# Rotating the columns of an 8192 x 8192 fp32 matrix: the wrapped row ends staged through SBUF as 512 B blocks

## The chip, the core and the metric

One NeuronCore of a Trainium2 chip. The time is the device time of one execution in microseconds (us); the figure of a kernel is the median of its runs.

## The reference

`x` is 8192 x 8192 float32, `shift` is 100, and the result is `np.roll(x, shift, axis=1)`: in every row, `out[r, c] = x[r, (c - 100) mod 8192]`. So a row of the output begins with the last 100 elements (400 B) of the input row, and goes on with its first 8,092 (32,368 B). A row is 32,768 B, the matrix 268.4 MB. Nothing is computed; every byte is read once and written once.

## The kernel before

It consists of DMAs from DRAM to DRAM and has no tile in SBUF. With `s = 100` it cuts the 8,192 rows into 16 chunks of 512 rows. For each chunk line 28 issues one DMA of the long pieces, `out[r, 100:] <- x[r, :8092]`: 512 pieces of 32,368 B, one a row. The chunks take turns between the queue of SP (`nc.sync`) and that of ACT (`nc.scalar`), 8 DMAs each. Line 30 issues, on GpSimd's queue, the row ends of the same chunk, `out[r, :100] <- x[r, 8092:]`: 512 pieces of 400 B, 16 DMAs in all.

No two DMAs touch the same bytes, so nothing in the data orders them. The only waits are those by which a semaphore that tells a DMA's completion is used again: the program as built lets four DMAs be outstanding on SP and on ACT and eight on GpSimd, and a later issue waits for the DMA that used its semaphore last. In the output row the long piece starts at byte 400 and ends at the row's end; in the input row it starts at byte 0. The row end starts at byte 32,368 of the input row and byte 0 of the output row.

Of the kernel before, what the change touches and what calls it, by code (L numbers as in the profile page):

```python
# [1 line left out]

# [4 lines left out]


@with_exitstack
def kernel(  # L10
    ctx: ExitStack,
    tc: tile.TileContext,
    x: bass.AP,
    shift: int,
    out: bass.AP,
):
    nc = tc.nc
    n_rows, n_cols = x.shape
    s = shift % n_cols

    engines = [nc.sync, nc.scalar]
    n_chunks = 16
    rows = n_rows // n_chunks
    for i in range(n_chunks):
        r = slice(i * rows, (i + 1) * rows)
        engines[i % 2].dma_start(out=out[r, s:], in_=x[r, :n_cols - s])
        if s > 0:
            nc.gpsimd.dma_start(out=out[r, :s], in_=x[r, n_cols - s:])  # L30


# [1 line left out]
_INS = ['x', 'shift']  # L34
_OUTS = [((8192, 8192), 'float32')]

_NUMBERS = {'shift': 100}


def kernel(**inputs):  # L40
    import numpy as _np
    import concourse.bacc as _bacc
    import concourse.tile as _tile
    from concourse import mybir as _mybir
    from concourse.bass_utils import run_bass_kernel_spmd as _run

    nc = _bacc.Bacc("TRN2", target_bir_lowering=False, num_devices=1)  # L47
    arrays, args = {}, []
    for name in _INS:
        if name in _NUMBERS:  # L50
            args.append(_NUMBERS[name])
            continue
        a = _np.ascontiguousarray(inputs[name])
        if a.dtype.kind in "iu":
            a = a.astype(_np.int64)
        arrays[f"in_{name}_dram"] = a
        args.append(nc.dram_tensor(f"in_{name}_dram", a.shape, _mybir.dt.from_np(a.dtype), kind="ExternalInput").ap())
    for i, (shape, dtype) in enumerate(_OUTS):
        dt = _mybir.dt.from_np(_np.dtype(dtype))
        args.append(nc.dram_tensor(f"out_{i}_dram", shape, dt, kind="ExternalOutput").ap())  # L60
    with _tile.TileContext(nc) as tc:  # L61
        kernel(tc, *args)
    r = _run(nc, [arrays], core_ids=[0])
    got = tuple(r.results[0][f"out_{i}_dram"] for i in range(len(_OUTS)))
    return got[0]
```

## Time and profile before

| what | value |
|---|---|
| median of 5 runs | 831.17 us (830.85 to 843.72) |
| the profiled execution, its own time | 828.21 us |
| its span, first to last instruction | 826.4 us |
| DMA share between 230 and 800 us | 1.00, at 331 GB/s |
| DMA share between 800 and 826.4 us | 0.57, at 232 GB/s |
| issue of a GpSimd DMA (L30) | 0.62 us each, 16 of them, the last at 114.2 us |
| issue to landing, median: SP, ACT, GpSimd | 399.3, 399.0, 107.6 us |

The span is that of one execution; its own time is 1.8 us more, and the median of the runs 4.8 us more. The page gives each DMA queue's share of the 16 DMA engines' time, the share of that time in which they were busy, and the bytes moved per second; GB/s count a copied byte once, though it is read and written. A queue's packet is what an engine takes from it in one turn: one long piece, or several short ones. The packet records of the trace, which the page adds up, give each packet's start, size and duration. "Issue to landing" of a DMA includes its waiting behind those that were issued before it.

### The profile page before, as it was taken

The numbers are of one execution on the slowest core, as the hardware profiler recorded it, in microseconds if no ns is written. First come the engines' busy times: TensorE is split into PE (matmuls) and PEld (weight loads), VectorE is DVE, ScalarE is ACT, GpSimd is POOL, SyncE is SP. The second block draws the span as 40 slices with busy tenths as digits, with TensorE's granted clock in tenths as the row PEclk, the third lists the DMA queues.
The fourth block names the chain that finished last, engine by engine and source line by source line (L and its number), as shares of the span: only waits on it lengthen the run. The fifth ranks groups of instructions, "written<-read, shape, count | busy, mean of one in ns | idle before, by whom it ended". The sixth has DMA issues, their size and how long they took to land. (4 is left out here: it accounts for less than half of the span.)

```text
span 826.4 us, 81 instructions
## 1 busy us (share of the span) xinstructions
POOL 10.2 (1%) x20
## 2 busy tenths in 40 slices
POOL 2000000000000000000000000000000000000000
DMA  9999999999999999999999999999999999999994
GB/s 292 319 319 326 321 314 325 332 318 332 325 331 329 343 327 332 334 321 332 335 323 337 335 331 334 327 335 334 331 332 327 329 332 329 324 326 331 334 323 213
DMA packets 9472, 268.44 MB, mean 325 GB/s; under 512 B 512, under 2 KB 512, under 8 KB 1280
## 3 DMA queue, kind: packets, MB, share of 16 engines
q1 hardware_dynamic: 4224, 132.58, 49.1%
q10 hardware_dynamic: 4224, 132.58, 47.0%
q0 software_dynamic: 1024, 3.28, 2.3%
HBM read 268.44 MB, written 268.44 MB: 650 GB/s over the span
## 5 line engine op out<-in xcount | busy, mean ns | idle before, releaser
L30 POOL DMA_DIRECT2D out_dram<-in_x_dram x16 | 10.0, 630 | 104.4 <-DMA out_dram<-in_x_dram 103.6
L47 POOL MEMSET const-float32-0.0<- 128x1 f32 x1 | 0.1, 98 | 0.2 <-issue 0.2
L47 POOL MEMSET const-bfloat16-1.0<- 128x1 bf16 x1 | 0.1, 101 | 0.0
L47 POOL MEMSET const-float32-1.0<- 128x1 f32 x1 | 0.1, 98 | 0.0
L47 POOL MEMSET const-uint8-127<- 128x1 uint8 x1 | 0.1, 98 | 0.0
## 6 DMA issues: line engine op xcount, KB each, us to landing
out_dram<-in_x_dram SPq DMA_DIRECT2D x8, 16184.0 KB, 399.3
out_dram<-in_x_dram ACTq DMA_DIRECT2D x8, 16184.0 KB, 399.0
out_dram<-in_x_dram POOLq DMA_DIRECT2D x16, 200.0 KB, 107.6
```

The source lines that it names most:

```text
L30: nc.gpsimd.dma_start(out=out[r, :s], in_=x[r, n_cols - s:])
L47: nc = _bacc.Bacc("TRN2", target_bir_lowering=False, num_devices=1)
```

## The change

The long pieces start at the next multiple of 128 elements: with `a = 128` and `g = a - s = 28`, line 31 of the new kernel copies `out[r, 128:] <- x[r, 28:8092]`, 8,064 elements (32,256 B) a row, in the same 16 DMAs on SP and ACT. The first 128 elements of an output row, the 100 wrapped ones and the 28 that stood at the front of the input row, go through SBUF. They lie apart in one input row, but the last 100 elements of row r - 1 and the first 28 of row r are neighbours in memory, so one read of 512 B fetches both. The rows are handled in 8 blocks of 1,024 (128 partitions x 8 rows). For each block GpSimd's queue issues a read of 1,024 such pieces (line 65), and a small read of the end of the eighth row of each partition (line 66); the first block, which has no row ahead of it, reads 1,024 ends of 400 B (line 59) and 1,024 fronts of 112 B (line 61). Two VectorE copies per block (lines 68 and 70) put the end and the front of the same row together in a second tile, and a DMA on GpSimd's queue (line 73) stores 1,024 blocks of 512 B to `out[:, :128]`. Each of the two pools has 8 buffers, as many as there are blocks. In the source the store of block k - 1 comes after the read of block k.

As the program is built, GpSimd's queue holds 25 DMAs in this order: L59, L61, L65, L66, L65, L73, L66, L73, L65, L66, L73, and then L65, L66, L73 for each further block, with the last store at the end. Each L73 waits for VectorE's copies of its block, each copy for the landing of what it reads; from the ninth DMA on, an issue also waits for the DMA eight places ahead of it.

```diff
-    for i in range(n_chunks):
-        r = slice(i * rows, (i + 1) * rows)
-        engines[i % 2].dma_start(out=out[r, s:], in_=x[r, :n_cols - s])
-        if s > 0:
-            nc.gpsimd.dma_start(out=out[r, :s], in_=x[r, n_cols - s:])
+    a = -(-s // 128) * 128
+    g = a - s
+    for i in range(n_chunks):
+        r = slice(i * rows, (i + 1) * rows)
+        if a < n_cols:
+            engines[i % 2].dma_start(out=out[r, a:], in_=x[r, g:n_cols - s])
...
+    m = 8
+    n_st = n_rows // P // m
+    reads = ctx.enter_context(tc.tile_pool(name="reads", bufs=n_st))
+    heads = ctx.enter_context(tc.tile_pool(name="heads", bufs=n_st))
+    xt = x.rearrange("(k p j) c -> k p j c", j=m, p=P)
+    ot = out.rearrange("(k p j) c -> k p j c", j=m, p=P)
+    tiles = []
+    for k in range(n_st + 1):
+        if k < n_st:
+            t = reads.tile([P, m + 1, a], x.dtype)
+            if k == 0:
+                nc.gpsimd.dma_start(out=t[:, 1:, :s], in_=xt[k, :, :, n_cols - s:])
+                if g > 0:
+                    nc.gpsimd.dma_start(out=t[:, :m, s:], in_=xt[k, :, :, :g])
+            else:
+                lead = bass.AP(tensor=x.tensor, offset=k * P * m * n_cols - s,
+                               ap=[[m * n_cols, P], [n_cols, m], [1, a]])
+                nc.gpsimd.dma_start(out=t[:, :m, :], in_=lead)
+                nc.gpsimd.dma_start(out=t[:, m, :s], in_=xt[k, :, m - 1, n_cols - s:])
+            h = heads.tile([P, m, a], x.dtype)
+            nc.vector.tensor_copy(h[:, :, :s], t[:, 1:, :s])
+            if g > 0:
+                nc.vector.tensor_copy(h[:, :, s:], t[:, :m, s:])
+            tiles.append(h)
+        if k > 0:
+            nc.gpsimd.dma_start(out=ot[k - 1, :, :, :a], in_=tiles[k - 1])
```

## The prediction

> **What bounds the kernel now.** I read the page's head and its DMA part first, because no compute engine does anything here.
>
> ```profile
> span 826.4 us, 81 instructions
> ...
> DMA  9999999999999999999999999999999999999994
> GB/s 292 319 319 326 321 314 325 332 318 332 325 331 329 343 327 332 334 321 332 335 323 337 335 331 334 327 335 334 331 332 327 329 332 329 324 326 331 334 323 213
> DMA packets 9472, 268.44 MB, mean 325 GB/s; under 512 B 512, under 2 KB 512, under 8 KB 1280
> ## 3 DMA queue, kind: packets, MB, share of 16 engines
> q1 hardware_dynamic: 4224, 132.58, 49.1%
> q10 hardware_dynamic: 4224, 132.58, 47.0%
> q0 software_dynamic: 1024, 3.28, 2.3%
> HBM read 268.44 MB, written 268.44 MB: 650 GB/s over the span
> ```
>
> The 16 DMA engines are busy from the first slice to the last one. The long pieces (q1 is one of the SP and ACT queues, q10 the other) take 96.1% of the engines' time, the row ends on GpSimd's q0 2.3%. So a long piece costs 0.961 x 826.4 x 16 / 8192 = 1,551 ns, and all row ends together cost 0.023 x 826.4 = 19.0 us of every engine. The sum closes: 0.984 x 826.4 = 813.2 us of work, and 13 us in which an engine has nothing (2 us of start, the rest in the last slices, where the engines end one after the other).
>
> Second, the rate by stage, where the columns are POOL's busy time, the clock, the DMA share and GB/s:
>
> ```profile
> 0.00:114.00 114.00, 9.59 (x19) 1.00 0.99 316
> 114.00:230.00 116.00, 0.62 (x1) 1.00 1.00 324
> 230.00:800.00 570.00, 0.00 (x0) 1.00 1.00 331
> 800.00:826.40 26.40, 0.00 (x0) 1.00 0.57 232
> ```
>
> While row ends are in flight the engines are as busy, but move less: (331-316)/331 x 114 + (331-324)/331 x 116 = 7.6 us are lost, on top of the 9.9 us that 3.28 MB take at 331 GB/s. Together 17.5 us, close to q0's 19.0: the time of small pieces is nearly all added to the end, and only 1.5 to 2 us come back because the long pieces run a little faster beside them.
>
> Third, how GpSimd's ring gets its turns, from the timeline of the issues:
>
> ```profile
> 0.74 214.04 SPq L28 DMA_DIRECT2D out_dram<-in_x_dram  x5
> 0.74 219.62 ACTq L28 DMA_DIRECT2D out_dram<-in_x_dram  x5
> 1.26 5.03 POOL L30 DMA_DIRECT2D out_dram<-in_x_dram  x8 [0.82 <-PEq L61]
> 19.39 0.62 POOL L30 DMA_DIRECT2D out_dram<-in_x_dram  x1 [13.10 <-DMA out_dram<-in_x_dram]
> 33.00 0.62 POOL L30 DMA_DIRECT2D out_dram<-in_x_dram  x1 [12.98 <-DMA out_dram<-in_x_dram]
> ```
>
> One 200 KB DMA completes every 13.6 us. On each engine it is 32 pieces, which the packet records of the trace show as three packets (11, 11 and 10 pieces of 400 B) and a 4-byte completion: four turns, each beside one long piece of either other queue, 2 x 1.55 + 0.3 = 3.4 us. 4 x 3.4 = 13.6. The chain of waits follows POOL only, to 115 us, so it says nothing of the end; the end is the engines' total work.
>
> **What the change does to that sum.** (1) Removed: all sixteen 400 B DMAs, -19.0 us (q0's share).
>
> (2) The long pieces shrink from 32,368 to 32,256 B: 0.35% of 0.961 x 826.4 = 794 us, -2.7 us. They now start at 512 B of the output row instead of 400, but at byte 112 of the input row instead of 0. Does that change their rate? The trace has only the old form. The shortest long packets in its records take 1,199 ns, 27.0 GB/s, with the write at byte 400: an unaligned write alone doesn't hold an engine back. The mean is 1,551 because 16 engines together ask for more than they get. Here the Trainium skill's "HBM Reference" (Specifications) speaks against a gain: it puts a stack at about 716 GB/s. Our row of 331 GB/s is 331 read and 331 written, 662 in total, so by the page at most 716/662 = 8% (about 60 us) is left for any alignment; by the row nothing is shown to be left. Bounds: -60 us, and +16 us (2%) if an unaligned read costs more than an unaligned write did, since the change moves the offset rather than removing it. I take 0, the row's side: both ends of the copy still differ by 400 B.
>
> (3) Added: the reads into SBUF. The first block of 1,024 rows has 1,024 pieces of 400 B and 1,024 of 112 B; seven more have 1,024 of 512 B and 128 of 400 B each: 10,112 pieces, 4.55 MB. (4) Added: 8 stores of 1,024 blocks of 512 B: 8,192 pieces, 4.19 MB. In all 8.75 MB instead of 3.28 and 18,304 pieces instead of 8,192. The old packets closed at about 4 KB, so 8 blocks of 512 B should make one. Per engine the first block is then 6 + 2 packets, the seven others 8 + 1 each, the stores 8 each: 8 + 63 + 64 = 135 packets, instead of 48.
>
> Price of a packet: the nearest row is q0's own: 19.0 us / 48 = 396 ns for 4,267 B on average. The shortest records of that form take 155 to 172 ns, 25.7 GB/s. So 135 packets cost between 135 x 0.165 = 22 us and 135 x 0.385 = 52 us. The excess of about 220 ns arises in a copy with HBM on both sides; a read into SBUF or a store out of it has HBM on one side only. I take half the excess: 165 + 110 = 275 ns, 37 us. A rule speaks for less: the skill's "DMA: Bandwidth & Descriptors" (Specifications) asks for 512 B or more for line rate and says that below it the engine reads, modifies and writes. By that rule the old 400 B were the dear form, and 8.75 MB / 16 at 27.0 GB/s, 20 us, would be the whole new price; the sum would be 19.0 + 2.7 - 20 = 2 us faster. The row doesn't show that penalty: 400 B pieces reach 25.7 GB/s in the shortest packets, and the mean's excess of 220 ns is smaller than the long packets' own, 1,551 - 1,199 = 352 ns. I stay with 37.
>
> (5) Relief: small packets that use HBM on one side leave more of it to the long ones. Before, 19 us of small packets gave back about 2 us. 37 us of packets with half the demand should give back about three times that: 6, so 4 more.
>
> Sum: -19.0 - 2.7 + 37 - 4 = +11 us. Span 826.4 + 11 = 838. The profiled execution's own time was 828.21 and the median of the runs 831.17; the same difference on the median gives 842.
>
> **What I cost at nothing, and its cover.** VectorE's 16 copies have no row before. GpSimd's fills of one element took 0.1 us; an estimate from the 0.96 GHz in the skill's page "VectorE: DVE Perf Modes" (Specifications) is 800 / 0.96 = 0.8 us for the larger copy, up to 15 us in all. GpSimd issues 25 DMAs instead of 16, at 0.62 us for 512 pieces; with twice the pieces up to 1.3 us, some 30 us. Each store waits in GpSimd's queue for the copies of its block, and so for that block's read. Behind the waiting store stands the read two blocks later, and for that VectorE and then the next store wait. This is a chain, but by the built order the next block's reads are already in the ring when a store waits: about 10 turns of work cover the copies. Turns: 135 + 25 completions = 160 x 3.4 = 544 us (the same count gives 64 x 3.4 = 218 for before, where the rows above show the small pieces gone by 230). The long pieces run to about 815 us. So 270 us of cover is left; a stall of 5 us at each of eight stores uses 40 of it. SP and ACT keep their 16 issues and their waits.
>
> **The rivals.** (A) *Hidden anyway, no change.* If HBM alone is the limit, the engine time of the SBUF legs is absorbed: its bytes are unchanged at 537 MB, 811 us at 662 GB/s, plus 10 to 13 us of start and tail: span 822 to 824, median 827 to 829. For it: 662 is near the page's 716, and long packets at 1,199 show that engines could do more. Against it: the 316 row, where small pieces gave back only 2 of 19 us.
>
> (B) *Faster.* The price is hidden in the long pieces' 1,551 ns, at their write starting at byte 400. To come out over 1% faster in spite of the +11, the long pieces must gain 19 of 794 us: from 1,551 to about 1,513 ns. With 4%, 32 us, the time is 810. For it: the mean is far above 1,199. Against it: the unaligned long pieces already move 662 GB/s, and 112 B of offset remain on the read. The alignment then did not do what it says.
>
> (C) *Much slower.* Small packets cost as much as before or more (0.385 us or above): 52 - 19 - 2.7 - 2 = +28, 859. Also here: if a packet held one block, 1,060 turns x 3.2 us would outlast the long pieces, and the ring would end alone, well over 880. The 11-piece packets speak against that.
>
> **How the numbers follow.** The forecast has 0.44 (its own range 836 to 852), A 0.30, B 0.14, C 0.12. A change of 1%, about what a measurement of this kernel can tell from no change, is 823 and 839.5. Faster: B's 0.14, and 0.02 of A that ends below 823: 0.16. Same: the rest of A, 0.28, and 0.06 of the forecast that ends between 836 and 839: 0.34. Slower: 0.38 and C's 0.12: 0.50. For 8 in 10, the range leaves out the stronger half of B and the upper half of C: 815 to 862. The likeliest is 842.
>
> **What would show it.** q0's share near 37/838 = 4.4%: 2.5% supports the rule and A, 6% supports C. q1 plus q10 at 94 to 95% with a rate in the last undisturbed stage of 331: my zero for alignment; 340 or more is B, 325 or less an unaligned read that costs. The last store's issue near 500 to 550 us; after 800 it would be C's chain. VectorE under 2% busy. I am wrong if the long pieces' rate moves by over 1% either way, or if small packets fall outside 165 to 385 ns.

## The result and the profile after

The changed kernel takes 831.61 us in the median of 44 runs (822.99 to 845.26), the kernel before 835.44 us in 79 runs taken beside them. The ratio is 0.9959 with a 95% interval of 0.994 to 0.9977: 0.4% faster, about 3.4 us, inside the 1% that I had called no change. Forecast were 842 us, 11 us slower than before. In two later sets of runs the ratio was 0.9952 (0.9911 to 0.9992) and 0.9952 (0.9922 to 0.9983). A ratio leaves out the runs that took over 1.5% longer than the fastest of their kernel, so it differs from the quotient of the two medians, which is 0.9954 in the first set and 0.9983 and 0.9993 in the later ones. The level differs from set to set (the kernel before had medians from 835 to 854 us; 854 and 839 both on the chip numbered 0), so below only kernels of one set are compared; a percentage is turned into microseconds with the median of before in that set.

The profiled execution took 839.33 us (span 837.5); only seven of the 44 runs took longer, so the length of its end may not be typical. Its stages can be read. The page:

```profile
span 837.5 us, 111 instructions
...
q1 hardware_dynamic: 4224, 132.12, 45.7%
q10 hardware_dynamic: 4224, 132.12, 45.7%
q0 software_dynamic: 2544, 8.75, 5.4%
HBM read 268.79 MB, written 268.44 MB: 641 GB/s over the span
```

GpSimd's ring (its queue on the DMA engines, q0) grew from 2.3% to 5.4%: 0.054 x 837.5 = 45.2 us of every DMA engine, 26 more than before. But the long pieces fell from 96.1% to 91.4%, to 765.5 us, 1,495 ns each instead of 1,551. All work together is 0.968 x 837.5 = 811 us, before 813. The price of the small pieces was paid in engine time, and nearly all of it came back in the same place. What made this execution longer than before's is idle time, nearly all of it at the end, where the engines stop one after the other: 27 us against 13. By stage (the columns are VectorE's and GpSimd's busy time, the clock, the DMA share and GB/s):

```profile
0.00:114.00 114.00, 1.99 (x5) 8.04 (x14) 1.00 0.99 335
114.00:230.00 116.00, 1.43 (x3) 4.43 (x6) 1.00 1.00 338
230.00:500.00 270.00, 3.42 (x8) 6.25 (x8) 1.00 1.00 338
500.00:650.00 150.00, 0.00 (x0) 0.00 (x0) 1.00 1.00 330
650.00:800.00 150.00, 0.00 (x0) 0.00 (x0) 1.00 0.99 328
800.00:837.50 37.50, 0.00 (x0) 0.00 (x0) 1.00 0.37 152
```

The rate is higher while the small pieces are in flight, where before it was lower (316 and 324). GB/s count each byte that an engine moves, and a byte moved between DRAM and SBUF touches the memory once, a byte copied from DRAM to DRAM twice (the 268.79 MB read on the page are 264.24 MB of long pieces and 4.55 MB read into SBUF). The small pieces are 8.75 MB in some 530 us, 16.5 GB/s. So the memory carries 2 x 338 - 16.5 = 660 GB/s in the third row, and 2 x 330 = 660 in the fourth. The traffic at the memory is the same with the small pieces and without them.

The chain of the new stages did what the count of turns said. The timeline of the last block:

```profile
474.64 0.58 DVE L68 COPY h<-t 128x800 f32<-128x800 f32 x1 [7.27 <-DMA t<-in_x_dram]
475.51 0.86 POOL L73 DMA_DIRECT2D out_dram<-h  x1 [64.24 <-DVE h L68]
```

From the third block on each store waits 63 to 67 us for its block, and none of it shows: the engines stay fully busy, and the last store is issued at 475.5 us, some 360 us before the last long piece lands.

### The profile page after: what moved, and what is told of

It reads as the page before. It is cut to its first block, busy times and chain, and to the rows that moved or that the text cites. A ratio compares the mean times of both kernels' runs of the same rounds, so it can differ in the third digit from the quotient of the medians.

```text
span 837.5 us, 111 instructions
## 1 busy us (share of the span) xinstructions
DVE 6.8 (1%) x16; POOL 18.7 (2%) x28
## 3 DMA queue, kind: packets, MB, share of 16 engines
q0 software_dynamic: 2544, 8.75, 5.4%
HBM read 268.79 MB, written 268.44 MB: 641 GB/s over the span
## 4 chain that ended last, share of the span: by engine, by line
another core or an unknown queue 35%; issue 16%; DMA 5%; DVE 1%; POOL 0%; POOLq 0%; PEldq 0%
DMA t<-in_x_dram 5%; DVE h L68 0%; POOL out_dram L73 0%; DVE h L70 0%; POOL t L59 0%; POOLq L104 0%; POOL t L66 0%; POOL t L65 0%; PEldq L104 0%; POOLq L73 0%
## 5 line engine op out<-in xcount | busy, mean ns | idle before, releaser
L73 POOL DMA_DIRECT2D out_dram<-h x8 | 6.9, 865 | 456.6 <-DVE h L68 418.6
L65 POOL DMA_DIRECT2D t<-in_x_dram x7 | 6.3, 893 | 0.0
L68 DVE COPY h<-t 128x800 f32<-128x800 f32 x8 | 4.6, 578 | 108.1 <-DMA t<-in_x_dram 108.1
L70 DVE COPY h<-t 128x224 f32<-128x224 f32 x8 | 2.2, 278 | 360.2 <-DMA t<-in_x_dram 360.2
L66 POOL DMA_DIRECT2D t<-in_x_dram x7 | 3.9, 564 | 0.0
L59 POOL DMA_DIRECT2D t<-in_x_dram x1 | 1.0, 1033 | 0.8 <-PEq L104 0.8
L61 POOL DMA_DIRECT2D t<-in_x_dram x1 | 0.9, 897 | 0.0
```

The lines of the kernel that those rows point to most:

```text
L59: nc.gpsimd.dma_start(out=t[:, 1:, :s], in_=xt[k, :, :, n_cols - s:])
L61: nc.gpsimd.dma_start(out=t[:, :m, s:], in_=xt[k, :, :, :g])
L65: nc.gpsimd.dma_start(out=t[:, :m, :], in_=lead)
L66: nc.gpsimd.dma_start(out=t[:, m, :s], in_=xt[k, :, m - 1, n_cols - s:])
L68: nc.vector.tensor_copy(h[:, :, :s], t[:, 1:, :s])
L70: nc.vector.tensor_copy(h[:, :, s:], t[:, :m, s:])
```

## The experiments

Two theories. **M**: the memory's total of reads and writes sets the time, and a leg into or out of SBUF costs a DMA engine time that is hidden. **E**, the prediction's: each engine's packet times add up to the end. A third question is what alignment and block size are worth.

### The long pieces alone

`long_u` is before without line 30; `long_a` is after without everything below line 31; `long_b` is `long_a` with the read moved to byte 0.

```diff
 long_u:  out[r, 100:] <- x[r, 0:8092]      (no row ends)
 long_a:  out[r, 128:] <- x[r, 28:8092]     (no heads)
 long_b:  out[r, 128:] <- x[r, 0:8064]      (no heads)
```

> Before with the row ends left out (the first 100 columns of the output aren't written), long pieces at byte 400 as before. Two theories are told apart by this run and the next: M (the memory's read and write traffic, 662 GB/s in all, sets the time; a leg into or out of SBUF costs a DMA engine time that is hidden) and E (each engine's packet times add up to the end). M: 3.28 MB at 331 GB/s is 9.9 us, and the 7.6 us that the rate was short while row ends ran: -17.5 us. E: q0's share, -19 us. Both the same here; it is the base for the alignment and for the price of the row ends.

Measured: 830.92 us beside 853.85, ratio 0.9747 (0.9699 to 0.9794), -21.6 us. Somewhat more than either theory had.

> After with the heads left out (the first 128 columns of the output aren't written): long pieces from byte 112 of the input to byte 512 of the output. The changed kernel was 3 to 4 us faster than before. E: its q0 cost every engine 45 us, so without it the time is some 48 us below before. M: its q0 costs only its memory bytes, 4.19 MB at 331 GB/s = 12.7 us, so the time is some 16 us below before, and within 2 us of long_u. If alignment of the write gains anything by itself, long_a is below long_u by more than the 2.7 us of its smaller size.

Measured: 823.73 us, ratio 0.9661 (0.9617 to 0.9704), -28.9 us. In a later set (`long_a2`, below) -23.3. E, with -48, falls. But M's -16 is also missed: the heads cost more than their bytes. Against `long_u` it is 7.2 us faster, and its runs (822 to 828) lie below all of `long_u`'s (829 to 837). 2.7 us of this are the smaller size; 4.5 us, 0.5%, are left for writing at byte 512 instead of 400. This rests on one set: the ratio of `long_a2`, 0.9722, lies near `long_u`'s 0.9747.

> Long pieces aligned on both sides: byte 0 of the input row to byte 512 of the output row, same size as long_a (the first 128 columns aren't written, and the rest is rotated by 128 instead of 100). If a byte offset on either side costs anything, this is faster than long_a by over 1% (8 us). M without any alignment effect: equal to long_a within 3 us.

Measured: 822.17 us, ratio 0.9632 (0.9581 to 0.9682). Within 1.6 us of `long_a`: the read's offset of 112 B costs nothing that shows.

### Engine time without memory traffic

`sb2sb` and `hbm2sb` are before with eight DMAs added on GpSimd's queue. They add work that the reference doesn't need, and change nothing in the output.

```diff
+    for k in range(8):
+        nc.gpsimd.dma_start(out=f1, in_=f0)                       # sb2sb: SBUF to SBUF, 4 MB
+        nc.gpsimd.dma_start(out=f1, in_=x[k * P:(k + 1) * P, :])  # hbm2sb instead: DRAM to SBUF, 4 MB
```

> Before with eight DMAs of 4 MB from SBUF to SBUF added behind the row ends on the GpSimd queue: 64 packets of 32 KB for each DMA engine, none of it touches the memory. At 27.0 GB/s they take 8 x 8 x 1.21 = 78 us of every engine. E: about 75 us slower than before. M: the engines would need only 698 us for all bytes at 27.0 GB/s, so at most 5 us slower.

Measured: 867.65 us beside 850.64, ratio 1.0227 (1.018 to 1.0274), +19 us. M had at most 5, E 75.

> The same with eight reads of 4 MB from DRAM into SBUF: as many bytes and packets for the engines, but 33.5 MB more read from memory. M: 33.5 MB at 662 GB/s, about 50 us slower than before. E: 78 to 99 us slower. The difference to the SBUF-to-SBUF run is what a memory leg costs.

Measured: 900.65 us, ratio 1.0574 (1.0516 to 1.0631), +49 us; M had 50, E 78 to 99. The page of `sb2sb` and its stages (the column for VectorE is there too; the added DMAs ran between about 215 and 520 us):

```profile
q1 hardware_dynamic: 4224, 132.58, 44.4%
q10 hardware_dynamic: 4224, 132.58, 43.7%
q0 software_dynamic: 2176, 36.83, 11.0%
```

```profile
230.00:500.00 270.00, 0.00 (x0) 3.70 (x7) 1.00 1.00 409
500.00:650.00 150.00, 0.00 (x0) 0.00 (x0) 1.00 1.00 343
650.00:800.00 150.00, 0.00 (x0) 0.00 (x0) 1.00 1.00 328
```

And the stages of `hbm2sb`:

```profile
230.00:500.00 270.00, 3.18 (x6) 1.00 1.00 370
500.00:650.00 150.00, 0.53 (x1) 1.00 1.00 341
650.00:800.00 150.00, 0.00 (x0) 1.00 1.00 323
```

q0 took 11.0% of the span of 862.6 us, 95 us, of which the old row ends are 17. The added 78 us of engine time cost 19. Why 19, and not nothing? The engines moved 409 GB/s in the first row, near the 16 x 27.0 = 432 that the shortest packets allow; in the packet records nearly three quarters of the long pieces took no more than 1,199 ns there, the shortest time of before. The SBUF copies took 33.5 MB in 305 us, 110 GB/s, so the long copies were left with 299 instead of 328: for those 305 us the engines were the limit, and (328-299)/328 x 305 = 27 us would be lost by this count, found after the run. In `hbm2sb` the reads took 33.5 MB in 340 us, 99 GB/s: the memory carried 2 x 370 - 99 = 641 GB/s there, and 2 x 323 = 646 after it. The same total, with reads alone added. So in these two runs a leg without memory is hidden until the engines reach their own ceiling, and a leg at the memory costs its bytes.

### Which leg of the heads costs

`reads_only` is after without line 73; `stores_only` has no reads and stores zeros. `long_a2` and `after_base` are `long_a` and after once more, in the same set.

```diff
 reads_only:
-            nc.gpsimd.dma_start(out=ot[k - 1, :, :, :a], in_=tiles[k - 1])
 stores_only (lines 57 to 66 and 68 to 70 removed):
+            nc.vector.memset(h, 0.0)
```

> After without heads again (the first 128 columns aren't written), as the base on the same chip for the next three. As before: 3.0 to 3.8% below the kernel before, runs within 6 us of each other.

Measured: 815.63 us beside 839.03, ratio 0.9722 (0.9678 to 0.9767); runs from 813 to 822.

> The changed kernel on the same chip, for the price of its heads: M by bytes alone 12.7 us above long_a; the earlier ratios, taken on different chips, say about 25 us. E: 45 us.

Measured: 838.48 us, ratio 0.9952 (0.9922 to 0.9983). The heads cost 0.9952 - 0.9722 = 2.3%, 19 us (23 by the medians). M by bytes had 12.7, E 45. The queues of `after_base` (span 839.6) and of `long_a2` (span 820.5), each followed by the stage from 500 us:

```profile
q10 hardware_dynamic: 4224, 132.12, 46.0%
q1 hardware_dynamic: 4224, 132.12, 45.6%
q0 software_dynamic: 2544, 8.75, 5.0%
...
500.00:650.00 150.00, 0.00 (x0) 0.00 (x0) 1.00 1.00 329
```

```profile
q1 hardware_dynamic: 4224, 132.12, 50.6%
q10 hardware_dynamic: 4224, 132.12, 48.2%
...
500.00:650.00 150.00, 0.00 (x0) 1.00 1.00 322
```

Busy are 0.966 x 839.6 = 811 us in the one and 0.988 x 820.5 = 811 in the other. The two executions differ by 19 us, and all of it is idle time: 28 us against 10. The bytes of the heads did not lengthen the busy time, because the copies ran faster in this kernel: 2 x 329 = 658 GB/s at the memory from 500 us on, when the heads were nearly done, against 2 x 322 = 644. So the memory's total is steady within a run, but differs by 1 to 2% from kernel to kernel. Why it is higher here is not shown.

> After without the stores of the heads (the first 128 columns aren't written; reads into SBUF and VectorE's copies stay). Price of the reads above long_a: M by bytes 4.55 MB / 662 GB/s = 7 us; E: about 22 us, half of q0's 45.

Measured: 832.69 us, ratio 0.9892 (0.9856 to 0.9928), 1.7% or 14 us above the base (17 by the medians), twice the price of the bytes.

> After without the reads (VectorE sets the tiles to zero, and they are stored, so the first 128 columns are zero). Price of the stores above long_a: M by bytes 4.19 MB / 662 GB/s = 6 us; E: about 20 us. If the two prices together are about 13 us and after's is 25, the rest comes from having both, that is from the chain or the spread of the engines at the end; if one leg is dear alone, it holds the rest.

Measured: 819.9 us, ratio 0.976 (0.9707 to 0.9813), 0.4% or 3 us above the base; with the intervals it can't be told from nothing, nor from its bytes' 6 us. The queues of `reads_only` (span 822.9) and of `stores_only` (span 817.6):

```profile
q1 hardware_dynamic: 4224, 132.12, 46.8%
q10 hardware_dynamic: 4224, 132.12, 46.7%
q0 software_dynamic: 1392, 4.55, 4.3%
```

```profile
q1 hardware_dynamic: 4224, 132.12, 48.9%
q10 hardware_dynamic: 4224, 132.12, 48.6%
q0 software_dynamic: 1152, 4.19, 1.3%
```

Nearly the same bytes, 4.3% against 1.3%: 35 us of engine time for the reads, 10.5 for the stores. In the packet records a store of eight 512 B blocks takes 162 ns on average, close to its shortest, 159. A read of eight takes 494 ns on average; two thirds take about the same 160, the rest up to 2,700. So on this ring small reads are held up beside the long copies and stores from SBUF aren't. Added up, the shares of `reads_only` are 97.8%, which leaves 18 us idle, those of `stores_only` 98.8%, 10 us, as `long_a2` has. These profiles can't say what makes up the 14 us that the reads cost: the profiled execution of `reads_only` was only 2 us longer than that of `long_a2`, with 6 us less busy time and 8 us more idle time.

### Block size and staging of the row ends

```diff
 staged400 (before's long pieces; blocks of 1,024 rows as in after, no VectorE):
+            nc.gpsimd.dma_start(out=t, in_=xt[k, :, :, n_cols - s:])
+            nc.gpsimd.dma_start(out=ot[k - 1, :, :, :s], in_=tiles[k - 1])
 direct512 (after's long pieces):
+        nc.gpsimd.dma_start(out=out[r, :128], in_=x[r, n_cols - 128:])
 direct2 (after's long pieces):
+        nc.gpsimd.dma_start(out=out[r, :s], in_=x[r, n_cols - s:])
+        nc.gpsimd.dma_start(out=out[r, s:128], in_=x[r, :28])
```

> Before with one thing changed: the 400 B row ends go through SBUF (8 reads of 1,024 pieces and 8 stores of 1,024 pieces on the GpSimd queue), no VectorE, no 512 B blocks, long pieces at byte 400 as before. E: 96 packets instead of 48, 16 to 19 us slower than before. M, if the 7.6 us lost beside the old row ends came from copying small pieces from memory to memory: 4 to 7 us faster than before. M, if they came from the size or place of the 400 B writes[...]: the same as before within 2 us.

Measured: 850.85 us beside 853.85, ratio 0.9935 (0.9897 to 0.9973), -5.5 us, as M has it if copying small pieces from memory to memory made the loss. Staging alone gives about what the whole change gives.

> After's long pieces, and the first 128 columns written by direct DRAM-to-DRAM copies of 512 B a row, to aligned addresses (they take the last 128 columns of the input row, so the data of those columns is not the reference's). The block size and place of the change without its SBUF staging. If writes below 512 B made the loss of 7.6 us beside the old row ends: 3 to 6 us faster than before. If copying small pieces from memory to memory made it: 64 packets instead of 48, the same as before or up to 4 us slower.

Measured: 840.8 us beside 850.64, ratio 0.9857 (0.9801 to 0.9914), -12 us, twice what I expected even for the block size; the 7.6 us of the old row ends and the 4.5 that `long_a` gained by the aligned write make 12.1, a sum made after the run.

> After's long pieces, with row ends (400 B) and fronts (112 B) each copied directly DRAM to DRAM, no SBUF. Two small pieces a row instead of one. If small writes are dear: 5 to 15 us slower than before. If only the number of packets counts (64 instead of 48): 0 to 4 us slower.

Measured: 854.78 us, ratio 1.0072 (1.0044 to 1.0101), +6 us. Between the two forms of the expectation, at the lower end of "small writes are dear". The stages of `staged400`, of `direct512` (an execution of 851.5 us) and of `direct2`:

```profile
50.00:230.00 180.00, 6.69 (x8) 1.00 1.00 331
...
500.00:650.00 150.00, 0.00 (x0) 1.00 1.00 324
```

```profile
50.00:230.00 180.00, 3.73 (x6) 1.00 1.00 322
...
500.00:650.00 150.00, 0.00 (x0) 1.00 1.00 320
```

```profile
50.00:230.00 180.00, 9.96 (x16) 1.00 1.00 307
230.00:500.00 270.00, 2.50 (x4) 1.00 1.00 321
500.00:650.00 150.00, 0.00 (x0) 1.00 1.00 325
```

Only `direct2` slows down while its small pieces are in flight (307 against 325), as before did (316 against 331). Direct copies of 512 B don't (322 and 320), nor do 400 B through SBUF: 6.55 MB in some 370 us are 18 GB/s, so 2 x 331 - 18 = 644 at the memory, and 2 x 324 = 648 without them. So the loss belongs to copies from DRAM to DRAM in pieces of under 512 B, or to such copies off the multiples of 512 B: the small pieces of `direct512` start at such multiples on both sides, those of before and `direct2` don't, and no run separates size from place. Either escape removes the loss, aligned 512 B or SBUF; the change uses both. Why the 400 B stores of `staged400` don't pay is not shown here.

### The rings and the rows

`ends_hw` is before with line 30 on the queue of its chunk's long pieces; `after_hw` is after with all DMAs on SP and ACT; `after_ilv` gives each DMA engine every sixteenth row.

```diff
 ends_hw:
-            nc.gpsimd.dma_start(out=out[r, :s], in_=x[r, n_cols - s:])
+            engines[i % 2].dma_start(out=out[r, :s], in_=x[r, n_cols - s:])
 after_hw (two of its changes):
-                nc.gpsimd.dma_start(out=t[:, :m, :], in_=lead)
+            nc.sync.dma_start(out=t[:, :m, :], in_=lead)
...
-            nc.gpsimd.dma_start(out=ot[k - 1, :, :, :a], in_=tiles[k - 1])
+        nc.scalar.dma_start(out=ot[k, :, :, :a], in_=tiles[k])
 after_ilv:
-            engines[i % 2].dma_start(out=out[r, a:], in_=x[r, g:n_cols - s])
+            engines[i % 2].dma_start(
+                out=out[r, a:].rearrange("(j e) c -> e j c", e=16),
+                in_=x[r, g:n_cols - s].rearrange("(j e) c -> e j c", e=16))
```

> The changed kernel beside the next three, and a second profile of it. M (the memory's traffic sets the time, SBUF legs are hidden): the rate of the copy while heads are in flight equals the rate after them within 1%, as in the first profile, and the ratio to before is 0.994 to 0.998. The first profile had 25 us of idle time at the end, before's 13; if the spread between DMA engines at the end is a cost of the small pieces on the third ring, idle time here is again above the 9 us of the runs without small pieces; if it was chance, 9 to 13.

Measured: 848.15 us beside 849.56 (836 to 859 in 22 runs). The rate is 335 with heads (50 to 230 us) and 326 or 327 after them (from 500 us); at the memory 2 x 335 - 16.5 = 654 and 2 x 326.5 = 653, the same again. Its shares, 46.3, 46.3 and 5.3%, leave 2.1% of 838.8, 18 us, idle: more than in the runs with long pieces alone, less than in the first profile.

> Before with one thing changed: each chunk's 400 B row ends are issued on the queue of its long pieces (SP or ACT, right behind them), so GpSimd's ring isn't used; same pieces, places and bytes. If the third ring lets the DMA engines drift apart, and so makes the late end and the spread of the runs: about 8 us faster than before, idle time at the end near 9 us, the runs within 6 us of each other, as in the runs with long pieces alone. If not: within 3 us of before.

Measured: 852.12 us, ratio 1.0076 (1.0039 to 1.0113): not the 8 us faster of the first form, and the same as before within 1%. The idle end is indeed short (99.3% of 854.5 are busy, 6 us idle), but the rate was between 313 and 320 all along, and its runs still lie 12 us apart.

> After with one thing changed: in each DMA of long pieces, DMA engine e gets rows e, e+16, e+32, ... instead of 32 rows in a run, so that the 16 engines work 32 KB apart instead of 1 MiB apart. Same pieces and bytes. If 331 GB/s is all that the memory gives to a copy: within 4 us of after. If it comes from the engines meeting in the same parts of the memory: long pieces well under 1,550 ns (down to 1,199), and 2 to 15% faster.

Measured: 844.57 us, ratio 0.9991 (0.9957 to 1.0024), its interval overlapping after's, and 322 to 325 GB/s after the heads. Whether the engines stand 32 KB or 1 MiB apart in the matrix is not what holds the rate.

> After's pieces, all on SP's and ACT's queues: the reads into SBUF first on SP, the stores on ACT behind two chunks of long pieces, GpSimd's ring not used. M: the same bytes, so at most the tail can differ: with the third ring as the cause of the drift some 8 to 10 us faster than after; else within 4 us of it. E: no different from after.

Measured: 848.35 us, ratio 1.0027 (1.0007 to 1.0047), the same as after within 1%. But its 22 runs lie within 7 us (845 to 852), after's in the same set within 23. The two pages, after's second profile (span 838.8) and `after_hw`'s (span 846.2), the latter with two of its stages:

```profile
DMA packets 10992, 272.99 MB, mean 325 GB/s; under 512 B 640, under 2 KB 640, under 8 KB 2800
...
q10 hardware_dynamic: 4224, 132.12, 46.3%
q1 hardware_dynamic: 4224, 132.12, 46.3%
q0 software_dynamic: 2544, 8.75, 5.3%
```

```profile
DMA packets 27137, 272.99 MB, mean 323 GB/s; under 512 B 3585, under 2 KB 18945, under 8 KB 18945
...
q10 hardware_dynamic: 12544, 136.32, 49.5%
q1 hardware_dynamic: 14592, 136.67, 49.3%
...
50.00:230.00 180.00, 6.47 (x16) 0.00 (x0) 1.00 0.98 319
...
650.00:800.00 150.00, 0.00 (x0) 0.00 (x0) 1.00 1.00 324
```

With everything on two rings the engines end together (98.8% busy, 10 us idle, against 18), and the time repeats. What that gives, the busy time takes back: 836 us against 821. On SP's and ACT's queues each small piece is a packet of its own, 27,137 packets instead of 10,992. And here their engine time was not hidden: in the packet records they moved 38 GB/s between 50 and 230 us, so the memory carried 2 x 319 - 38 = 600 GB/s there, against 2 x 324 = 648 later. They came twice as densely as on GpSimd's ring (17 GB/s) and in another order, so which of ring, packet form and density makes the loss isn't shown. M's hidden legs are shown for GpSimd's ring only. No version that I ran and that computes the reference is clearly better than the changed kernel; `staged400`, at 0.9935, is its equal with less code.

## Why the prediction was wrong, step by step

**The removal and the size (steps 1 and 2)** stood: 19.0 us of engine time went.

**Alignment taken as zero (2)** was nearly right. In the trace the rate after the heads is 330 and 328 instead of 331. The long pieces alone show a gain of 0.5%, 4.5 us, for the write, in one set, and none for the read.

**The count of packets (3, 4)** stood: 135 data packets an engine, 8 of the 512 B blocks in one, the last store at 475.5 us against 500 to 550, copies of 0.58 us against an estimate of 0.8. Two counts were off without consequence: GpSimd's queue holds 24 DMAs, not 25 (so 159 turns and not 160), and one piece a packet, in C, would be 1,144 turns and not 1,060. **Their price** was off: 45 us instead of 37. I halved the excess over both legs alike; nearly all of it lies in the reads (494 ns in `reads_only`), hardly any in the stores (162 in `stores_only`).

**The relief (5) is the step that failed.** I took 6 us in all, 4 of them new. The long pieces gave back 794 - 765.5 = 28.5 us, of which 2.7 are their size. With 26 in place of 4 and 45 in place of 37 the sum is -19 - 2.7 + 45 - 26 = -3 us; measured were -3.4. This sum is of busy time alone. The idle time, 13 us in before's profile, the prediction carried over unchanged, without a reason; three profiles of after have 27, 18 and 28 us. That -3 comes so near to -3.4 is therefore in part luck. The price of the small pieces was hidden as rival A had it: the engines wait for the memory, and while one is busy with SBUF the others get its share. The signs that were to tell A from C looked at engine time, and so pointed the wrong way: q0's 5.4% is nearer to C's 6% than to A's 2.5%, and yet A, with its 2 to 4 us faster, is what happened.

Why did I give A only 0.30? I read the 316 of the first stage as proof that small pieces add their engine time. It was the penalty of direct copies of small unaligned pieces, which the change removes: `direct512` and `staged400` keep their small pieces and show no dip. The page "DMA: Bandwidth & Descriptors" of the Trainium skill (Specifications), with its 512 B, had pointed to it, and I set it aside because the shortest 400 B packets were quick. The shortest packet shows what an engine can do alone; it can't show what a piece does to the memory that all share. For copies from DRAM to DRAM the runs agree with the page (307 GB/s with pieces below 512 B, 322 with 512 B), though they don't separate size from place; for stores out of SBUF (`staged400`) they show no such cost. Likewise the 662 GB/s beside the 716 of "HBM Reference" (Specifications) were in the text, and I used them to bound the alignment and not to ask what an engine's waiting is worth.

**Where the gain went.** The penalty removed is worth the 7.6 us of the prediction's second excerpt, the aligned write 4.5 (in one set). Against this the reads cost 14 us, 7 more than their bytes. With the stores' 3 us, the smaller long pieces' 2.7 and the bytes of the old row ends, 9.9, the account is -7.6 - 4.5 - 2.7 - 9.9 + 14 + 3 = -8. Measured are -3.4 to -4.1 in three sets; `long_u` gave 21.6 for the row ends where 7.6 and 9.9 stand here, and after's heads cost 19 us together where the two legs alone cost 17, so the account isn't closed to better than some 4 us. In the profile of `after_base` the whole price of the heads is idle time at the end. That this comes with GpSimd's ring is supported by `after_hw` (10 us idle against 18), which changes the order and the form of the packets as well; that it comes with the small reads is supported by one profile each of `reads_only` and `stores_only` (18 and 10 us idle). Against both stands `direct2`: it had small copies on that ring and 8 us idle, though its 22 runs lie 19 us apart. How an engine falls behind stays open.

## What to carry to other kernels

Before adding up the time of DMA packets, ask what the packets wait for: convert the rate into traffic at the memory (a DRAM-to-DRAM byte counts twice), and if it is the same in every stage, cost an edit by its bytes there, and expect the engine time of legs through SBUF to be hidden up to the engines' own ceiling (shown here on GpSimd's ring only). Then look at the end of the run, where the engines may stop further apart: in `after_base` the price of the heads stood there. A dip in a mixed stage says only that something is dear there; which property makes it dear needs a second form of the same piece. On GpSimd's ring the small reads were the dear leg and the small stores were not; on SP's and ACT's, one piece a packet, both took about 30 ns a piece.

## What the runs showed of the hardware beyond that

On GpSimd's ring eight 512 B pieces went as one packet of 159 ns at best; on SP's and ACT's each was a packet of its own, 25 ns at best and 29 to 31 on average. The long copies held about 640 to 664 GB/s of reads and writes together in every stage without direct copies of small unaligned pieces, except where the engines were near their ceiling (`sb2sb`, 409 of 432 GB/s) and beside the small packets of `after_hw`. In one set 22 runs of after lay within 23 us and 22 runs of the same pieces on two rings within 7.
